# Prompt's squares moved earlier on ScalarE, and one two-bank PSUM tile for the transposes of both attention heads

## The chip, the cores and the metric

The kernel runs on one core of a Trainium2 chip. The metric is the device time of one execution in microseconds. Before the change the median of three runs was 2239.68 us (2239.0 to 2242.85). What follows rests on one profiled execution of the kernel before.

Engine names are those of the profile: PE (TensorE), PEld (its weight loads), DVE (VectorE), ACT (ScalarE), POOL (GpSimd), SP (SyncE, which issues the DMAs).

## The reference, cut to what matters

One layer of a hybrid encoder runs over two groups of tokens with the same weights: a prompt of 512 tokens and a sample of 1024.

```
h = rms_norm(x, norm1_g)                  # x * rsqrt(mean(x*x) + eps) * g
z = h @ w_in                              # conv, pooling, short conv, q, k, v, gates
pooling branch: windowed means of z_b over time, minus z_b;
                p = einsum(p, pool_w) * pool_scale
attention:      s = q k^T + bias on an 8-row by 16-column neighbourhood
                o = softmax(s) v
x = x + (sum_i sigmoid(gate_i) * branch_i) @ w_o
x = x + (val * silu(gate)) @ w_down       # from rms_norm(x, norm2_g) @ w_up
y = rms_norm(x, final_g)
```

Everything is float32; a product is made of three matmuls over a high and a low part of each operand.

## The kernel before, in words

Tokens are cut into three chunks of 512: chunk 0 is the prompt, chunks 1 and 2 the sample. Channels stand on the 128 partitions, so x of one chunk is eight tiles of 128x512 (index k). `split` (L113 to L115) makes the high part with an ACT copy or cast and the low part with a DVE subtraction; `mm3` (L121 to L125) issues the three matmuls of one product, L123, L124 and L125.

**The opening stage.** ACT and DVE split the first weights and prompt's x (`rh`, `rl`). `more_w` (L368) loads and splits two more weight tiles (`m0`, `m1`), and the loop over t the two raw tiles of the value weights into `vwh` and `vwl` (L400 to L405), each of which is made of a half from either raw tile. `square` (L381 to L388) squares one x tile on ACT and adds it to a running sum on POOL (on DVE for chunk 1 and k over 4); the sums are `sq` of a chunk for k 0 to 3 and for k 4 to 7. `rms_scale` (L138 to L152) has PE add these over the partitions with matmuls one column wide (`rb`, L142), then DVE makes the reciprocal root with ten small operations on 128x4 (`rs_v`, `rs_y`, `rs_t`), and a diagonal tile `dg`; `spread` (L156) sends that through PE to all partitions. PE meanwhile multiplies prompt's unnormalised x by the four query and key weights (`zt`), then by the value weights (`zv`, four tiles of 24 matmuls), and scales afterwards. The sample's chunks are normalised first (`norm`, L423 to L426).

**The middle stage.** A plan (L555 to L813) lists twelve column tiles of `w_in`; each is 24 matmuls (`z`) for each of the chunks 1, 2 and 0, followed by an evacuation. Between the z tiles `pump` (L548) puts attention's steps, 24 in all: 4 column blocks of 3 query blocks for 2 pairs of heads. A step makes for each of its two heads the scores `s` on PE, adds the bias and takes the maximum on DVE (L615), exponentials on ACT (L621), a reciprocal on DVE, the scaling on ACT (L624), two or three transposes on PE into a PSUM tile `tp` (L627), and the split into `ph` and `pl`; then PE multiplies by the values (`o`, L634 to L636). The pooling branch (L678 to L725) evacuates its z tiles into `xb`, makes windowed sums on DVE over 1,560 or so columns (`pa`, `pb`), and PE multiplies each chunk by `pool_w` (`pm`, L720); ACT scales that into `ob`. There are two such branches, the second with two levels of sums more.

**PSUM.** Eight banks of 128x512: here four for `z` in rotation (`ztile`), two for `s` and `o`, and two in the pool `mps`, used in turn by `tp` and `pm`.

**The order.** The program is written in one order, and a list scheduler then lays out one queue for each engine, with its own idea of when each operand and buffer is ready; `tc.high_priority()` puts some parts ahead. Each engine works off its queue as laid out.

Of the kernel before, what the change touches and what calls it, by code (L numbers as in the profile page):

```python
# [12 lines left out]
F32 = mybir.dt.float32  # L13
# [4 lines left out]
PSUM = bass.MemoryType.PSUM  # L18
# [46 lines left out]
def encoder(ctx, tc, xT, w_in, w_out, w_o, w_up, w_dn, par, rrel, outT):  # L65
# [122 lines left out]
    with ExitStack() as outer:  # L188
# [140 lines left out]
        with ExitStack() as pha:  # L329
# [59 lines left out]

            more_w(0, 13, HD**-0.5)  # L390
            for k in range(4):
                load_x(k, 1)
            more_w(1, 15, None)
            SP.dma_start(pt, par[:, NG:])
            for k in range(4, KT):
                load_x(k, 1)
            for k in range(KT):
                square(k, 1)
            vw = [[tt(f"vw{m}{a}", F32R) for a in range(4)] for m in "hl"]
            for t in range(2):  # L400
                raw = wp.tile([P, DM], F32, tag="wraw", name=f"wr_v{t}")
                SP.dma_start(raw, w_in[16 + t])
                for a in range(4):
                    hi, lo = (vw[m][a].rearrange("p (k t d) -> p k t d", k=2, t=2)[:, :, t, :] for m in range(2))
                    split(hi, lo, raw[:, a * 256 : (a + 1) * 256].rearrange("p (k d) -> p k d", k=2))  # L405
            for k in range(KT):
                square(k, 0)
            for k in range(KT):
                load_x(k, 2)

# [116 lines left out]
        with ExitStack() as p1:  # L527
                open_zps(4)
                sps = pool(p1, "sps1", 2, space=PSUM)
                mps = pool(p1, "mps1", 2, space=PSUM)  # L530
                bigp = pool(p1, "bigp", 3, side="right")
                gop = pool(p1, "gop", 5, side="right")
                att = p1.enter_context(ExitStack())
# [29 lines left out]
                def attention_pair(p):  # L563
                    t = {}

                    def step(base, r0, kr0, nk, rmi, j):
                        qh, ql, kh, kl, R = (t[x] for x in ("qh", "ql", "kh", "kl", "R"))
                        nt = nk // 4
                        n = nk * 32
                        qc = (base + r0 * GW) // C  # L570
                        qcols = slice(qc * C + j * P, qc * C + (j + 1) * P)
                        k0 = base + kr0 * GW
                        nm = f"{p}{qc}{j}"
                        if j == 0:
                            t["ot"] = ap.tile([P, C], F32, tag="ot", name=f"ot{p}{qc}")
                        ot = t["ot"]

                        def win(x):
                            return x[:, k0 : k0 + nk * GW].rearrange("p (r c) -> p r c", c=GW)[
                                :, :, CB[j] : CB[j] + 32  # L580
                            ]

                        vv = ap.tile([P, 3, 2 * P], F32R, tag="vv", name=f"vv{nm}")
                        g0 = k0 // GW
                        for r in range(4):
                            SP.dma_start(
                                vv[r * 32 : (r + 1) * 32, :nt].bitcast(F32),
                                vt_d[g0 + r : g0 + nk : 4, CB[j] : CB[j] + 32, p * 2 * P : (p + 1) * 2 * P].rearrange(
                                    "i c d -> c i d"
                                ),  # L590
                            )

                        ph = ap.tile([P, 3, 2, P], F32R, tag="ph", name=f"ph{nm}", bufs=1)
                        pl = ap.tile([P, 3, 2, P], F32R, tag="pl", name=f"pl{nm}", bufs=1)
                        for hh in range(2):
                            rows = slice(hh * HD, (hh + 1) * HD)
                            sp = sps.tile([P, C], F32, tag="s", name=f"s{nm}{hh}")
                            so = sp[:, :n]
                            PE.matmul(so, qh[rows, qcols], win(kh)[rows], start=True, stop=False)
                            PE.matmul(so, qh[rows, qcols], win(kl)[rows], start=False, stop=False)  # L600
                            PE.matmul(so, ql[rows, qcols], win(kh)[rows], start=False, stop=True)
                            bm = ap.tile([P, 12, 32], F32, tag="bm", name=f"bm{nm}{hh}")
                            bmv = bm[:, :nk, :]
                            t0 = (kr0 - r0 + 4) * 31 + (CB[j] - 16 * j + 16)
                            rv = R[:, hh, t0 : t0 + 31 * nk]
                            rv = bass.AP(rv.tensor, rv.offset, [list(rv.ap[0]), [31, nk], [1, 32]])
                            cm = pcols("cm", 32 * j, 32)
                            G.tensor_tensor(bmv, rv, cm[:, None, :].broadcast_to([P, nk, 32]), ALU.add)  # L608
                            if rmi is not None:
                                rm = pcols("rm", 12 * rmi, 12)  # L610
                                G.tensor_tensor(bmv, bmv, rm[:, :, None].broadcast_to([P, nk, 32]), ALU.add)
                            s = ap.tile([P, 384], F32, tag="s", name=f"se{nm}{hh}")
                            sv = s[:, :n]
                            mx = small.tile([P, 1], F32, tag="mx", name=f"mx{nm}{hh}")
                            V.tensor_tensor_reduce(  # L615
                                sv, so, bmv.rearrange("p a b -> p (a b)"), 1.0, -3e38, ALU.add, ALU.max, mx
                            )
                            nmx = small.tile([P, 1], F32, tag="nmx", name=f"nx{nm}{hh}")
                            V.tensor_scalar(nmx, mx, -1.0, None, ALU.mult)
                            sm = small.tile([P, 1], F32, tag="sm", name=f"sm{nm}{hh}")  # L620
                            S.activation(sv, sv, AF.Exp, bias=nmx, accum_out=sm)  # L621
                            ri = small.tile([P, 1], F32, tag="ri", name=f"ri{nm}{hh}")
                            V.reciprocal(ri, sm)
                            S.activation(sv, sv, AF.Copy, scale=ri)  # L624
                            tp = mps.tile([P, C], F32, tag="m", name=f"tp{nm}{hh}")
                            for i in range(nt):
                                PE.transpose(tp[:, cols(i)], s[:, cols(i)], ident)  # L627
                            tv = tp[:, :n].rearrange("p (t q) -> p t q", q=P)
                            split(ph[:, :nt, hh, :], pl[:, :nt, hh, :], tv)
                        o = sps.tile([P, C], F32, tag="s", name=f"o{nm}")  # L630
                        ov = o[:, 0:256]
                        for i in range(nt):
                            a, b = (x[:, i].rearrange("p a b -> p (a b)") for x in (ph, pl))
                            PE.matmul(ov, vv[:, i, :P], a, start=(i == 0), stop=False)  # L634
                            PE.matmul(ov, vv[:, i, :P], b, start=False, stop=False)
                            PE.matmul(ov, vv[:, i, P:], a, start=False, stop=(i == nt - 1))  # L636
                        for hh in range(2):
                            rows = slice(hh * HD, (hh + 1) * HD)
                            dst = ot[rows].rearrange("p (r c) -> p r c", c=GW)[:, :, 16 * j : 16 * j + 16]
                            src = o[rows, hh * P : (hh + 1) * P].rearrange("p (r c) -> p r c", c=16)  # L640
                            (S.copy if hh else V.tensor_copy)(dst, src)

                        if j == 3:
                            SP.dma_start(bs_d[3, p, qc], ot)

                    def start():
                        for n in "qk":
                            for m in "hl":
                                t[n + m] = (qp if n == "q" else kp).tile([P, T], F32R, tag=n, name=f"{n}{m}{p}")
                                SP.dma_start(t[n + m].bitcast(F32), qk_d[n, p, m])  # L650
                        t["R"] = ap.tile([P, 2, RL], F32, tag="R", name=f"R{p}", bufs=1)
                        SP.dma_start(t["R"], rrel[p])

                    then(start)
                    kinds = [(0, 0, 0, 8, None), (SEQ_P, 0, 0, 12, 0), (SEQ_P, 8, 4, 12, 1)]
                    for kd in kinds:
                        for j in range(4):
                            then(lambda kd=kd, j=j: bg.append(lambda: step(*kd, j)))
# [19 lines left out]
                def pool_branch(i):  # L678
# [14 lines left out]
                    def sums():  # L693
# [22 lines left out]
                            )  # L716
                        pw = pcols("pw", i * P, P)
                        for c in range(NC):
                            m = mps.tile([P, C], F32, tag="m", name=f"pm{i}{c}")
                            PE.matmul(m, pw, s_lo[:, OFF[c] : OFF[c] + C], start=True, stop=True)  # L720
                            o = go(f"ob{i}{c}")
                            S.activation(o, m, AF.Copy, scale=pc("ps", i))
                            SP.dma_start(bs_d[1, i, c], o)
# [703 lines left out]
```

## Time and profile before

| what | value |
|---|---|
| median of three runs | 2239.68 us |
| the profiled execution | 2238.61 us |
| its span | 2236.8 us |
| PE busy | 2192.5 us, 98% |
| DVE busy | 1353.6 us, 61% |
| ACT busy | 774.7 us, 35% |
| POOL busy | 613.7 us, 27% |
| mean granted clock of PE | 0.992 |

Busy time of PE is a sum over instructions that overlap, so the pitch from one start to the next tells more than a duration. The granted clock is 1.00 at 2.4 GHz and 0.50 at 1.2 GHz. In a timeline, the bracket at the end of a row is the idle time of the engine before it and what ended it.

### The profile page before, as it was taken

Reading aid. Unit: us, or ns where it says so; the run is one execution under the profiler, and the core shown is the slowest. Engines: PE = TensorE matmul, PEld = TensorE weight load, DVE = VectorE, ACT = ScalarE, POOL = GpSimd, SP = SyncE. Lnnn points to the kernel's source line nnn. Section 1 sums busy time; section 2 is a strip of 40 time slices with the busy share of each in tenths; the row PEclk is TensorE's granted clock in tenths of the full one; section 3 lists DMA queues with packets and bytes.
Section 4 is the critical chain, followed back from the end, with each engine's and each line's share of the span. In section 5 each row is a group of like instructions: output and inputs, shape, how many; then the busy total and the mean of one; then the engine's idle time right before and its main releaser. Section 6 shows DMA issues by size and latency. Waiting matters only on the chain.

```text
span 2236.8 us, 26947 instructions
## 1 busy us (share of the span) xinstructions
PE 2192.5 (98%) x9898; PEld 1785.0 (80%) x9898; DVE 1353.6 (61%) x1968; ACT 774.7 (35%) x1316; POOL 613.7 (27%) x701
## 2 busy tenths in 40 slices
PE   8999999999999999999998999999999999999997
PEld 6886767888888778787876888888888887888886
DVE  6635553466666542778158988888777875341414
ACT  5335453333333353303133433333333334221112
POOL 3113343211211210353234544444334430000001
PEclk9999999999999999999998999999999999999999
DMA  5482322622322323874434111211111225432221
GB/s 206 172 294 68 124 77 79 237 84 87 118 79 92 104 99 117 291 252 141 125 112 153 58 67 66 66 57 62 67 62 52 67 80 184 141 123 58 88 86 48
DMA packets 112564, 253.89 MB, mean 114 GB/s; under 512 B 12848, under 2 KB 23600, under 8 KB 109360
## 3 DMA queue, kind: packets, MB, share of 16 engines
q1 hardware_dynamic: 112432, 252.17, 33.6%
q8 instruction: 78, 1.28, 0.2%
q14 instruction: 54, 0.44, 0.1%
HBM read 167.44 MB, written 84.68 MB: 113 GB/s over the span
## 4 chain that ended last, share of the span: by engine, by line
PE 51%; DVE 2%; issue 0%; POOL 0%; ACT 0%; POOLq 0%; DVEq 0%; ACTq 0%
PE yp L124 5%; PE yp L125 5%; PE yp L123 5%; PE ppu L123 4%; PE ppu L124 4%; PE ppu L125 4%; PE o L124 2%; PE o L125 2%; PE o L123 2%; PE p3T L124 1%; PE p3T L123 1%; PE p3T L125 1%; PE p1T L124 1%; PE p1T L125 1%; PE p1T L123 1%; PE p22T L125 1%
## 5 line engine op out<-in xcount | busy, mean ns | idle before, releaser
L123 PE MATMUL yp<-fs,wdhi 128*128 128x512 f32 x480 | 187.2, 392 | 2.4 <-ACT fs L114 2.4
L124 PE MATMUL yp<-fs,wdhi 128*128 128x512 f32 x480 | 188.0, 392 | 0.3 <-DVE fs L115 0.3
L125 PE MATMUL yp<-fs,wdlo 128*128 128x512 f32 x480 | 187.7, 391 | 0.0
L115 DVE TENSOR_TENSOR fs<-fr,fs 128x512 fp32r<-128x512 f32 x63 | 43.4, 691 | 180.0 <-ACT fs L114 180.0
L1198 POOL TENSOR_TENSOR u<-u,u 128x512 f32<-128x512 f32 x63 | 97.6, 1549 | 193.9 <-DVE u L1191 136.3
L847 DVE SCALAR_TENSOR_TENSOR acc<-glu,pt,acc 128x1552 f32<-128x1552 f32 x60 | 109.8, 1830 | 0.7
L1291 POOL TENSOR_TENSOR x<-x,rs 128x256 f32<-128x256 f32 x11 | 7.6, 725 | 371.1 <-DVE acc L1279 367.5
L123 PEld LDWEIGHTS yp<-fs,wdhi 128*128 128x128 f32 x480 | 90.2, 188 | 22.1 <-ACT fs L114 2.8
L114 ACT CAST fs<-fr 128x512 fp32r<-128x512 f32 x63 | 39.0, 621 | 197.7 <-PE yp L125 103.1
L124 PEld LDWEIGHTS yp<-fs,wdhi 128*128 128x128 f32 x480 | 90.6, 189 | 20.0 <-DVE fs L115 1.0
L125 PEld LDWEIGHTS yp<-fs,wdlo 128*128 128x128 f32 x480 | 90.7, 189 | 19.1
L1191 DVE SCALAR_TENSOR_TENSOR u<-c,pt,u 128x512 f32<-128x512 f32 x88 | 100.4, 1179 | 0.0
L253 POOL TENSOR_TENSOR Sg<-wr_g 128x512 f32<-128x512 f32 x16 | 21.4, 1335 | 285.3 <-DMA wr_g<-in_w_in 158.4
L1190 DVE SCALAR_TENSOR_TENSOR u<-c,pt,u 128x512 f32<-128x512 f32 x88 | 86.9, 1025 | 0.0
L608 POOL TENSOR_TENSOR bm<-R,pt 128x384 f32<-128x384 f32 (+1 forms) x48 | 48.0, 1002 | 122.6 <-DVE mx L615 113.5
L1197 ACT ACTIVATE u<-u 128x512 f32<-128x512 f32 x66 | 41.8, 634 | 112.5 <-DVE u L1191 112.5
L123 PE MATMUL z<-hh,wh_i 128*128 128x512 f32 x192 | 78.3, 408 | 0.0
L124 PE MATMUL y<-bl,wh_wo 128*128 128x512 f32 x192 | 75.4, 393 | 2.8 <-DVE bl L115 2.8
L124 PE MATMUL z<-hl,wh_i 128*128 128x512 f32 x192 | 76.3, 398 | 0.0
L125 PE MATMUL z<-hh,wl_i 128*128 128x512 f32 x192 | 76.3, 398 | 0.0
L124 PE MATMUL o<-ml,wh_o 128*128 128x512 f32 x192 | 75.1, 391 | 1.2 <-DVE ml L115 1.2
L123 PE MATMUL o<-mh,wh_o 128*128 128x512 f32 x192 | 75.4, 392 | 0.0
(511 smaller groups left out, 6572.4 us busy)
## 6 DMA issues: line engine op xcount, KB each, us to landing
g<-gate_d SPq DMA_DIRECT2D x24, 1024.0 KB, 5.3
wr_u<-in_w_up SPq DMA_DIRECT2D x44, 512.0 KB, 3.5
f_d<-u SPq DMA_DIRECT2D x66, 256.0 KB, 2.0
fr<-f_d SPq DMA_DIRECT2D x66, 256.0 KB, 2.7
wr_g<-in_w_in SPq DMA_DIRECT2D x32, 512.0 KB, 4.0
wdr<-in_w_dn SPq DMA_DIRECT2D x23, 512.0 KB, 3.5
gate_d<-gp SPq DMA_DIRECT2D x32, 256.0 KB, 2.0
x<-in_xT SPq DMA_DIRECT2D x24, 256.0 KB, 5.8
```

What stands on the lines that cost most here:

```text
L114: S.copy(hi, src)
L115: V.tensor_tensor(lo, src, hi.bitcast(F32), ALU.subtract)
L123: PE.matmul(ps, w[0][:, ws], x[0], start=first, stop=False, **kw)
L124: PE.matmul(ps, w[0][:, ws], x[1], start=False, stop=False, **kw)
L125: PE.matmul(ps, w[1][:, ws], x[0], start=False, stop=last, **kw)
L253: G.tensor_tensor(t, x, y, op)
L608: G.tensor_tensor(bmv, rv, cm[:, None, :].broadcast_to([P, nk, 32]), ALU.add)
L847: keep(V.scalar_tensor_tensor(a, g, w, a, ALU.mult, ALU.add))
L1190: V.scalar_tensor_tensor(b, r[:, 0:C], pc("fc", f * 3), b, ALU.mult, ALU.add)
L1191: V.scalar_tensor_tensor(b, r[:, 2 : C + 2], pc("fc", f * 3 + 2), b, ALU.mult, ALU.add)
L1197: S.activation(ug, ug, AF.Silu)
L1198: (V if j == NJ - 1 else G).tensor_tensor(uv, uv, ug, ALU.mult)
```

## The change: what it does

In the opening stage the prompt's eight squares (`square(k, 0)`), which stood behind the splits of the value weights, now stand four behind the first and four behind the second of the `more_w` tiles, ahead of the squares of chunk 1.

In attention, the transposes of both heads of a step go into one tile `tp` of two banks, and stand together behind the softmax of both heads; the two splits follow. The pool `mps` then holds one such tile, and `pm` takes its PSUM tile from the four `z` banks.

```diff
             more_w(0, 13, HD**-0.5)
             for k in range(4):
+                square(k, 0)
+            for k in range(4):
                 load_x(k, 1)
             more_w(1, 15, None)
             SP.dma_start(pt, par[:, NG:])
             for k in range(4, KT):
                 load_x(k, 1)
+            for k in range(4, KT):
+                square(k, 0)
             for k in range(KT):
                 square(k, 1)
...
-            for k in range(KT):
-                square(k, 0)
             for k in range(KT):
                 load_x(k, 2)
...
-                mps = pool(p1, "mps1", 2, space=PSUM)
+                mps = pool(p1, "mps1", 1, space=PSUM)
...
+                        ss = []
                         for hh in range(2):
...
                             S.activation(sv, sv, AF.Copy, scale=ri)
-                            tp = mps.tile([P, C], F32, tag="m", name=f"tp{nm}{hh}")
+                            ss.append(s)
+                        tp = mps.tile([P, 2, C], F32, tag="m", name=f"tp{nm}")
+                        for hh in range(2):
                             for i in range(nt):
-                                PE.transpose(tp[:, cols(i)], s[:, cols(i)], ident)
-                            tv = tp[:, :n].rearrange("p (t q) -> p t q", q=P)
+                                PE.transpose(tp[:, hh, cols(i)], ss[hh][:, cols(i)], ident)
+                        for hh in range(2):
+                            tv = tp[:, hh, :n].rearrange("p (t q) -> p t q", q=P)
                             split(ph[:, :nt, hh, :], pl[:, :nt, hh, :], tv)
...
-                            m = mps.tile([P, C], F32, tag="m", name=f"pm{i}{c}")
+                            m = ztile(f"pm{i}{c}")
```

No instruction is added or taken away on any engine; their order changes. On PE, at the end of the first pooling branch, this stands before the change (z_2 belongs to the column tile that follows the branch, s and tp to attention, pm to the branch):

```order
L124 MATMUL z_2_2299<-hl_2_1072,wh_i_1895 128x512
L125 MATMUL z_2_2299<-hh_2_1071,wl_i_1896 128x512
L123 MATMUL z_2_2299<-hh_2_1088,wh_i_1895 128x512
L124 MATMUL z_2_2299<-hl_2_1089,wh_i_1895 128x512
L720 MATMUL pm_2186<-pa_2172,pt 128x512
L720 MATMUL pm_2191<-pa_2172,pt 128x512
L720 MATMUL pm_2196<-pa_2172,pt 128x512
L599 MATMUL s_2264<-kh_1624,qh_1620 128x384
L600 MATMUL s_2264<-kl_1626,qh_1620 128x384
L601 MATMUL s_2264<-kh_1624,ql_1622 128x384
L125 MATMUL z_2_2299<-hh_2_1088,wl_i_1896 128x512
```

Between the end of the branch's own z_0 and this first pm stand 38 z matmuls of the next column tile (24 of z_1 and 14 of z_2). At the same place in the changed kernel, on PE (s_2126 is preceded by s_2109, and that by the end of z_0):

```order
L604 MATMUL s_2126<-kh_1624,ql_1622 128x384
L632 MATMUL tp_2143<-pt,se_2116 128x128 x3
L632 MATMUL tp_2143<-pt,se_2133 128x128 x3
L640 MATMUL o_2154<-ph_2107,vv_2102 128x256
L602 MATMUL s_2235<-kh_1624,qh_1620 128x384
L603 MATMUL s_2235<-kl_1626,qh_1620 128x384
L604 MATMUL s_2235<-kh_1624,ql_1622 128x384
L726 MATMUL pm_2180<-pa_2166,pt 128x512
L641 MATMUL o_2154<-pl_2108,vv_2102 128x256
```

Seven more o, the other two pm and then the 24 of z_1 follow. No z matmul of the next column tile stands ahead of the pm any more. It is the same at the second branch, where 55 z matmuls stood between z_0 and the first pm before, and none now.

On DVE in the opening stage, before the change, this stands around the small operations for chunk 1 (vwl is the low part of the value weights, from the raw tiles wr_v_328 and wr_v_338; rb_1 and rb_0 are PE's sums for the chunks 1 and 0):

```order
L115 TENSOR_TENSOR vwl_324<-wr_v_328,vwh_320 128x2x128
L388 TENSOR_TENSOR sq_14_309<-sq_14_309,sq_17_317 128x512
L115 TENSOR_TENSOR vwl_325<-wr_v_328,vwh_321 128x2x128
L115 TENSOR_TENSOR vwl_324<-wr_v_338,vwh_320 128x2x128
L145 TENSOR_SCALAR rs_v<-rb_1_480 128x4
L115 TENSOR_TENSOR vwl_326<-wr_v_328,vwh_322 128x2x128
L131 TENSOR_SCALAR rs_y<-rs_v 128x4
L115 TENSOR_TENSOR vwl_325<-wr_v_338,vwh_321 128x2x128
```

In the changed kernel, on DVE at the same place (the raw tiles are wr_v_350 and wr_v_360):

```order
L115 TENSOR_TENSOR vwl_347<-wr_v_350,vwh_343 128x2x128
L145 TENSOR_SCALAR rs_v<-rb_1_480 128x4
L145 TENSOR_SCALAR rs_v<-rb_0_508 128x4
L131 TENSOR_SCALAR rs_y<-rs_v 128x4
L115 TENSOR_TENSOR vwl_348<-wr_v_350,vwh_344 128x2x128
L131 TENSOR_SCALAR rs_y<-rs_v 128x4
L133 SCALAR_TENSOR_TENSOR rs_t<-rs_y 128x4
L115 TENSOR_TENSOR vwl_349<-wr_v_350,vwh_345 128x2x128
L133 SCALAR_TENSOR_TENSOR rs_t<-rs_y 128x4
L134 TENSOR_TENSOR rs_t<-rs_t,rs_v 128x4
L115 TENSOR_TENSOR vwl_346<-wr_v_360,vwh_342 128x2x128
```

The second half of the first value weights (the row that reads wr_v_360) stood ahead of the operations that wait for PE, and now stands behind nine rows of which the first waits for PE's sums of chunk 1; the small operations of both chunks alternate. Elsewhere: POOL's nine additions for the chunks 0 and 1 had chunk 1's three first and have them last; PE's sums rb_0 go ahead of all but one of rb_1; on SP the first raw value weights go ahead of the loads of chunk 1's x, where they stood behind four of them.

## Rows read from the trace of the kernel before

**Rows 1.** The page, part 1: busy time of PE.

```profile
PE 2192.5 (98%) x9898; PEld 1785.0 (80%) x9898; DVE 1353.6 (61%) x1968; ACT 774.7 (35%) x1316; POOL 613.7 (27%) x701
```

**Rows 2.** Waits of PE in the whole span: total us, times, longest us.

```profile
PE rb L142 <- POOL sq L388: 3.3, 1, 3.3
PE tp L627 <- ACT se L624: 2.7, 7, 0.6
PE pm L720 <- DVE pa L713: 0.2, 1, 0.2
```

**Rows 3.** Timeline of PE, opening stage: start us, us, instruction, [idle before <- releaser].

```profile
24.52 0.39 PE L123 MATMUL zt<-rh,m1h 128*128 128x512 f32 x1
24.75 0.39 PE L124 MATMUL zt<-rl,m1h 128*128 128x512 f32 x1
29.75 1.62 PE L142 MATMUL rb<-ones,sq 128*128 128x1 f32 x14
35.27 0.59 PE L142 MATMUL rb<-ones,sq 128*128 128x1 f32 x2 [3.32 <-POOL sq L388]
...
46.84 1.98 PE L156 MATMUL rb<-dg,ones 128*128 128x512 f32 x4
52.48 0.28 PE L465 MATMUL zv<-vwh,rl 128*128 128x256 f32 x1
52.60 0.39 PE L123 MATMUL zt<-hh,wh_q 128*128 128x512 f32 x1
53.41 0.49 PE L123 MATMUL zt<-hh,m0h 128*128 128x512 f32 x1 [0.42 <-DVE x L424]
54.64 0.50 PE L124 MATMUL zt<-hl,wh_q 128*128 128x512 f32 x1 [0.74 <-DVE hl L115]
```

**Rows 4.** Short windows, opening stage: busy times by engine, then PEclk, DMA share.

```profile
32.25:32.50 0.25, 0.00 (x0) 0.00 (x0) 0.25 (x1) 0.25 (x2) 0.17 (x2) 1.00 0.00 0
32.75:33.00 0.25, 0.00 (x0) 0.00 (x0) 0.25 (x1) 0.25 (x2) 0.25 (x1) 0.50 0.00 0
39.50:40.00 0.50, 0.50 (x5) 0.31 (x4) 0.43 (x3) 0.00 (x0) 0.18 (x1) 1.00 0.82 74
```

**Rows 5.** Timeline of ACT, opening stage.

```profile
16.13 1.15 ACT L118 ACTIVATE m0h<-wr_m 128x512 fp32r<-128x512 f32 x2 [1.30 <-DMA wr_m<-in_w_in]
29.82 4.26 ACT L383 ACTIVATE sq<-x 128x512 f32<-128x512 f32 x8
```

**Rows 6.** Timeline of POOL, opening stage.

```profile
21.83 4.03 POOL L388 TENSOR_TENSOR sq<-sq,sq 128x512 f32<-128x512 f32 x3 [21.39 <-ACT sq L383]
31.04 8.63 POOL L388 TENSOR_TENSOR sq<-sq,sq 128x512 f32<-128x512 f32 x6 [5.18 <-ACT sq L383]
```

**Rows 7.** Timeline of DVE, opening stage.

```profile
16.80 1.29 DVE L119 SCALAR_TENSOR_TENSOR m0l<-wr_m,m0h 128x512 fp32r<-128x512 f32 x2 [1.15 <-ACT m0h L118]
28.41 0.76 DVE L115 TENSOR_TENSOR vwl<-wr_v,vwh 128x256 fp32r<-128x256 f32 x2
32.53 1.23 DVE L131 TENSOR_SCALAR rs_y<-rs_v 128x4 int32<-128x4 int32 x1
41.69 0.17 DVE L131 TENSOR_SCALAR rs_y<-rs_v 128x4 int32<-128x4 int32 x1
```

**Rows 8.** Timeline of DVE, first pooling branch, its start and end.

```profile
205.22 0.69 DVE L687 TENSOR_TENSOR xb<-z,rbp 128x512 f32<-128x512 f32 x1 [1.10 <-PE z L125]
217.76 1.83 DVE L713 SCALAR_TENSOR_TENSOR pa<-pb,pt,xb 64x1552 f32<-64x1552 f32 x1
```

**Rows 9.** Timeline of PE where the first pooling branch ends.

```profile
219.77 2.97 PE L720 MATMUL pm<-pa,pt 128*128 128x512 f32 x6
```

**Rows 10.** Timeline of DVE, second pooling branch, its start and end.

```profile
264.70 0.69 DVE L687 TENSOR_TENSOR xb<-z,rbp 128x512 f32<-128x512 f32 x1 [1.11 <-PE z L125]
280.37 2.15 DVE L713 SCALAR_TENSOR_TENSOR pa<-pb,pt,xb 64x1552 f32<-64x1552 f32 x1
```

**Rows 11.** Timeline of PE where the second pooling branch ends.

```profile
282.57 1.98 PE L720 MATMUL pm<-pa,pt 128*128 128x512 f32 x4 [0.15 <-DVE pa L713]
```

## Prediction

> **What bounds the kernel now.** I read the busy times first: PE is busy for 98% of the span [rows 1]. So whatever makes PE wait lengthens the program by as much, and an edit off PE is worth only what PE waits for it. The second view is therefore the list of PE's waits [rows 2]. Two entries are what the two edits touch: 3.3 us once, for prompt's sums of squares on POOL, and 2.7 us in seven waits of transposes for ACT's scaling, none above 0.6 us. PE waits 0.2 us in all for the pooling branch. Third come the timelines of the opening stage and of the two pooling branches; fourth the order in which the changed kernel's instructions stand, since it decides what waits behind what.
>
> **The opening stage.** Before, PE starts its last 24 key matmuls at 24.52 us, 0.23 us apart, and then waits 3.32 us until 35.27 [rows 3], because POOL adds chunk 1's squares from 21.83 and prompt's only from 31.04 [rows 6], ACT having begun those at 29.82 [rows 5]. The wait costs more than itself: the granted clock, 1.00 at 32.25 to 32.50, stands at 0.50 (1.2 GHz) at 32.75 to 33.00 and is back at 1.00 at 39.5 [rows 4]. So PE works from 35.27 to about 39.4, some 4.1 us, at half speed, which costs half of that, 2.05 us.
>
> After, ACT can start prompt's squares when the first extra weights are done, at 16.13 + 1.15 = 17.28, with 4.26 / 8 = 0.53 us each [rows 5]. POOL starts when two are there, at 18.4, and adds nine times in a row, chunk 1 last. One addition is 4.03 / 3 = 1.34 to 8.63 / 6 = 1.44 us [rows 6], nine are 12.1 to 13.0, so chunk 1's sum is there at 30.5 to 31.4; I take 30.8. PE comes to it after 23 matmuls, at 24.52 + 23 x 0.23 = 29.8, and waits 1.0. Nine sums of 1.62 / 14 = 0.12 us [rows 3], one key and two value matmuls and the last seven sums follow: 1.0 + 0.3 + 0.3 + 0.8, so PE is through with both chunks' sums at 33.2.
>
> There a new wait stands, the one that the DVE order shows. The second half of the first value weights' low part is queued behind an operation that waits for PE's last sum, and PE's next matmul needs it. In between stand seven small operations, 0.2 us apart (0.17 each once POOL is quiet; 1.23 while it adds), and three low parts of 0.76 / 2 = 0.38 us [rows 7]: 1.4 + 1.1 = 2.5, with a semaphore 2.6. PE resumes at 35.8. The value matmuls are 0.12 us apart (52.48 to 52.60 [rows 3]); DVE delivers the further halves every 0.8 us for six of them, 0.72. The 46 left of the first two value tiles take 5.7. A wait of 2.6 after a wait of 1.0 and small sums is so near to the one of 3.3 that I charge the same clock loss, 2.05: PE is there at 43.6. The two spreads take 1.9 (1.98 in the row at 46.84), two value tiles 48 x 0.12 = 5.8, and chunk 1's products start at 51.3. Before they start at 52.60 and then wait 0.42 and 0.74 [rows 3], in effect 53.8; after, DVE has normalised chunk 1 by about 51, as PE gets there, so I count those waits as gone. Gain: 53.8 - 51.3 = 2.5 us. Its ends are 4.6 (no fall of the clock) and 0 (the clock falls, and POOL and the normalisation are 1.2 us later each).
>
> On SP the first raw value weights now stand ahead of chunk 1's loads and wait for a buffer until DVE's low part of the first extra weights is done, 16.80 + 1.29 = 18.09 [rows 7]. That holds the x loads, and ACT still waits for data there. It costs nothing as long as POOL is busy with prompt's sums, until 18.4 + 6 x 1.36 = 26.6; beyond that it moves the end one for one, inside the bound above.
>
> **Attention's transposes.** Same count, same operations, and mostly z matmuls between scores and transposes as before. The first head's split now waits for the transposes of both heads, but five more z matmuls stand between the last transpose and `o`, 5 x 0.23 = 1.2 us, which covers it. I count 0; from below, if all seven waits went, -2.7, and from above a rival.
>
> **The pooling branches.** Here `pm` takes a bank of `z`, and the order on PE has changed most: between the end of the branch's z_0 and its first `pm` nothing stands but a step of attention. `pm` needs the whole of DVE's windowed sums. Before, these run from 205.22 to 217.76 + 1.83 = 219.59 [rows 8], 14.4 us, and PE's first `pm` starts at 219.77 [rows 9]; the second time from 264.70 to 280.37 + 2.15 = 282.52, 17.8 us [rows 10], and `pm` at 282.57 [rows 11]. DVE's queue holds the same rows in that stretch after the change, give or take a 0.3 us copy and a 0.55 us low part, so the stretch stays 14.3 and 18.4 us long by my count. What hid it was PE's own work: 38 z matmuls, 38 x 0.23 = 8.6 us, and 55, 12.5 us. These now come after `pm`. The rest (scores, transposes, `o`) is the same on both sides, but at the first branch eight `o` also move behind the first `pm`, 0.9. Added: 8.6 + 0.9 - 0.3 = 9.2 us, and 12.5 + 0.5 = 13.0 us; together 22.2. Seen as idle time, PE should stand still for 11 to 15 us at each place, in pieces, each ended by attention's chain or by `pa`.
>
> So long a stop brings the clock down, as 3.3 us did. I charge what [rows 4] showed, 4.1 us of work at half speed after each: 2 x 2.05 = 4.1. `pm` is in that work. The ends are 0 and twice this.
>
> One rule decides whether this is a loss at all. The row at 35.27 [rows 3] shows PE waiting 3.32 us for a sum, with value matmuls behind it whose weights' first low parts DVE had finished at 28.41 + 0.76 = 29.2 [rows 7]: nothing overtook. The Trainium skill ("TensorE: Matmul & The Clock Gate", Step-by-step: what each phase is for) says the same, that weight loads may be pulled ahead while matmuls stay in program order. If they could pass, the z matmuls would fill the stop and only the opening gain would be left, about 2237 us; that is the second rival below.
>
> **The sum.** -2.5 + 22.2 + 4.1 = +23.8 us. The profiled execution took 2238.61 us, 1.07 below the median of the runs, so +23.8 makes 2262.4 of it and 2263.5 of the median. I predict 2263.5 us, 1.1% slower.
>
> **The rivals.**
> - *Every step pays.* With both heads in one tile, each of the 24 steps waits for the slower softmax and for six transposes, at the most that a wait costs now, 0.6 us [rows 2]: 24 x 0.6 = 14 us more, 2278. For it: the split has lost its overlap with the second head. Against: the extra z matmuls before `o`.
> - *The stop is worth nothing.* At the branches matmuls go past the waiting `pm`, or the sums on DVE are done when PE gets there, which decides as soon as they take less than the 2 to 3.5 us of attention work in between. Then only the opening's 2.5 is left: 2237, faster. For it: `pm` waits 0.2 us now. Against: that is so only because of 8.6 and 12.5 us of z work in front, and the row at 35.27.
> - *Half a stop.* DVE gets through the sums a third faster, as evacuations and weight splits come later with PE standing: 4.8 and 5.9 us less, 2253. Against: the order puts the same rows between the first and the last sum.
> - *The change doesn't do what it says.* ACT's squares stay bound by loads; then the opening gains 0: 2266, inside the range.
>
> **How the numbers follow.** Forecast (with the last rival in it) 0.74, every step 0.13, half a stop 0.09, nothing 0.04. The range: from no clock loss, the larger opening gain and 2 us less at the branches, +15.5, to twice the clock loss, no gain and 4 us of further waits, +35: 2255 to 2275. The measurement tells about 0.2%, 4.5 us, from no change. Faster by that needs the stop to be worth nothing and the larger gain, 0.03; within it 0.02; slower 0.95.
>
> **What would show it.** In the opening: POOL's nine additions without a gap from about 18.4 to 31; no wait for prompt's sums; a wait of about 2.6 us of a value matmul on a DVE low part; chunk 1's products from about 51. At the branches: PE's idle time 10 us or more twice between 195 and 290 us, with `pm` waiting for `pa`, and PEclk at 0.50 about there. I am wrong if `pm` waits less than 5 us at either place, if transposes wait more than 0.6 us in most steps, or if the time stays under 2250.

## The result, and the profile after

The changed kernel took 2268.5 us (median; 2265.4 to 2269.0), the kernel before 2240.1. The ratio is 1.0115, 95% interval 1.0103 to 1.0127: slower by 1.0 to 1.3% (the quotient of the two medians is 1.0127). Forecast were 2263.5 us and 2255 to 2275. The profiled execution's span is 2266.3 us, 29.5 more than before.

To see where these 29.5 us come from, I put the first start of the same tile of the two traces side by side (tile views, us):

| Tile | before | after | later by |
|---|---|---|---|
| first product of chunk 1 (zt) | 52.6 | 52.5 | -0.1 |
| xb of pooling branch 1 | 205.2 | 204.2 | -1.0 |
| xb of pooling branch 2 | 264.7 | 274.3 | +9.6 |
| first yg, behind all of attention | 410.5 | 435.0 | +24.5 |
| first y | 903.0 | 927.3 | +24.3 |
| first p1T | 1224.1 | 1253.3 | +29.2 |
| end of the span | 2236.8 | 2266.3 | +29.5 |

So the opening gave 1.0 us, the first branch cost 10.6 and the second 14.9, and 5.0 came in a part of the program where PE, DVE, ACT and POOL have their instructions in the same order in both traces.

The waits of PE after the change (whole program; who waited for whom, us in total, times, the longest) answer to [rows 2]:

```profile
PE tp L632 <- ACT se L627: 11.6, 6, 4.7
PE o L640 <- ACT ph L114: 3.9, 2, 2.2
PE pm L726 <- DVE pa L719: 2.7, 1, 2.7
PE zv L466 <- DVE vwl L115: 1.8, 1, 1.8
PE s L602 <- ACT ot L647: 1.4, 1, 1.4
PE rb L142 <- POOL sq L388: 1.4, 1, 1.4
```

PE's wait for POOL's sums shrank from 3.3 us (prompt's) to 1.4 (chunk 1's, which POOL now adds last), and a wait of 1.8 us for `vwl` is new. Transposes wait only six times, but for up to 4.7 us. These long waits are where the branches are. PE's busy time, granted clock and DMA traffic in the two windows of the branches, before and then after:

```profile
200.00:240.00 40.00, 38.19 (x182) 1.00 0.28 90
240.00:300.00 60.00, 59.13 (x280) 1.00 0.35 115
```

```profile
200.00:240.00 40.00, 30.59 (x135) 0.83 0.20 65
240.00:300.00 60.00, 50.04 (x218) 0.83 0.36 115
```

PE stands 9.4 us in the first window and 10.0 in the second (1.8 and 0.9 before), and what it does there it does partly at half clock. PE's rows with a wait, and `pm`, in branch 1 (start, us, line, operation, times, idle time before and its releaser) answer to [rows 9]:

```profile
207.25 0.44 PE L602 MATMUL s<-kh,qh 64*128 64x384 f32 x1 [1.40 <-ACT ot L647]
212.71 0.90 PE L632 MATMUL tp<-pt,se 128*128 128x128 f32 x3 [4.66 <-ACT se L627]
215.30 0.90 PE L632 MATMUL tp<-pt,se 128*128 128x128 f32 x3 [1.68 <-ACT se L627]
217.87 0.58 PE L640 MATMUL o<-ph,vv 128*128 128x256 f32 x1 [1.67 <-ACT ph L114]
219.63 2.07 PE L726 MATMUL pm<-pa,pt 128*128 128x512 f32 x2
222.81 1.88 PE L726 MATMUL pm<-pa,pt 128*128 128x512 f32 x4
```

And in branch 2, answering to [rows 11]:

```profile
278.85 0.90 PE L632 MATMUL tp<-pt,se 128*128 128x128 f32 x3 [3.38 <-ACT se L627]
281.04 0.90 PE L632 MATMUL tp<-pt,se 128*128 128x128 f32 x3 [1.29 <-ACT se L627]
284.19 0.58 PE L640 MATMUL o<-ph,vv 128*128 128x256 f32 x1 [2.24 <-ACT ph L114]
291.76 5.49 PE L726 MATMUL pm<-pa,pt 128*128 128x512 f32 x6 [2.68 <-DVE pa L719]
```

`pm` itself waits 0 and 2.7 us. The idle time stands in front of the attention rows between z_0 and `pm`, each waiting for its softmax; when they are through, `pa` is ready or nearly so. Read by `pm`'s own wait, the stop would look small.

The opening's PE rows after, answering to [rows 3]:

```profile
31.27 2.17 PE L142 MATMUL rb<-ones,sq 128*128 128x1 f32 x18 [1.35 <-POOL sq L388]
33.87 2.32 PE L142 MATMUL rb<-ones,sq 128*128 128x1 f32 x14
37.93 0.58 PE L466 MATMUL zv<-vwl,rh 128*128 128x256 f32 x1 [1.75 <-DVE vwl L115]
45.07 1.88 PE L156 MATMUL rb<-dg,ones 128*128 128x512 f32 x4
```

PE's busy time and, behind it, the granted clock there (the window's length stands first), answering to [rows 4]:

```profile
32.00:34.00 2.00, 2.00 (x18) 1.00 0.48 154
34.00:36.00 2.00, 2.00 (x15) 0.65 0.00 0
36.00:38.00 2.00, 0.25 (x2) 0.50 0.00 0
40.00:42.00 2.00, 2.00 (x14) 0.65 0.00 0
```

The clock fell at 34.6 us, while PE was busy with sums of one column and not in a wait, and was back at 41.4. In the kernel before it fell at 32.6, inside the wait.

### The profile page after: what moved, and what is told of

Same layout as the page of the kernel before. It is cut to its first block, busy times and chain, and to the rows that moved or that the text cites. A ratio compares the mean times of both kernels' runs of the same rounds, so it can differ in the third digit from the quotient of the medians.

```text
span 2266.3 us, 26927 instructions
## 1 busy us (share of the span) xinstructions
PE 2205.4 (97%) x9898; PEld 1795.9 (79%) x9898; DVE 1350.5 (60%) x1968; ACT 777.5 (34%) x1316; POOL 614.8 (27%) x701
## 3 DMA queue, kind: packets, MB, share of 16 engines
q1 hardware_dynamic: 112432, 252.17, 33.2%
## 4 chain that ended last, share of the span: by engine, by line
PE 49%; DVE 3%; issue 0%; POOL 0%; ACT 0%; POOLq 0%; DVEq 0%; ACTq 0%
PE yp L124 5%; PE yp L125 5%; PE yp L123 5%; PE ppu L125 3%; PE ppu L124 3%; PE ppu L123 3%; PE o L124 2%; PE o L125 2%; PE o L123 2%; PE p3T L124 1%; PE p3T L123 1%; PE p3T L125 1%; PE p1T L124 1%; PE p1T L125 1%; PE p1T L123 1%; PE p4B L125 1%
## 5 line engine op out<-in xcount | busy, mean ns | idle before, releaser
L123 PE MATMUL y<-bh,wh_wo 128*128 128x512 f32 x192 | 75.6, 395 | 1.2 <-DVE g L1006 1.2
```

Of the source, the lines that this page charges most:

```text
L123: PE.matmul(ps, w[0][:, ws], x[0], start=first, stop=False, **kw)
```

## The experiments

### The two parts apart

The squares alone, with attention and `pm` as before:

```
 more_w(0, 13, HD**-0.5)
+for k in range(4): square(k, 0)
...
 for k in range(4, KT): load_x(k, 1)
+for k in range(4, KT): square(k, 0)
...
-for k in range(KT): square(k, 0)
```

> The kernel before with the prompt's squares moved as in the change, and nothing else. Theory A (the opening gives what the trace after shows there): first product of chunk 1 no later, branch 1's STT chain about 1.0 us earlier than before, the time 2239 us (-1.0; between -2.5 and 0). Rival (the about 5 us that the trace after lost between 927 and 1253 us, where no order changed, come from the opening's part, by another layout of buffers or another phase of the clock): 2244 us, and y's first product to p1T's first row takes 326 us where before it took 321.

Measured: ratio 0.9988 (0.9978 to 0.9997), 2.7 us faster. It was run once more later:

> The first experiment (the prompt's squares moved, nothing else) run again beside these two, since its gain of 2.7 us stands near the noise. If the opening's gain is real: ratio 0.9975 to 0.9997, chunk 1's first product at 52 to 53 us (half-clock stretch of 6.6 us as in the changed kernel) or at 54.3 again (about 10 us). If it was chance: ratio 0.9997 to 1.001.

The second time: 0.9992 (0.9983 to 1.0000), 1.8 us. So the opening's part is worth about 2 us. Chunk 1 started at 54.3 and 56.2 us in these two traces and at 52.5 in that of the changed kernel, whose opening is the same, because the half-clock stretch lasted longer: 10.2 and 13.7 us for 6.8.

Attention's part alone (joint tile, `pm` from z's pool, squares as before):

```
-mps = pool(p1, "mps1", 2, space=PSUM)
+mps = pool(p1, "mps1", 1, space=PSUM)
...
-tp = mps.tile([P, C], F32, tag="m", name=f"tp{nm}{hh}")
+tp = mps.tile([P, 2, C], F32, tag="m", name=f"tp{nm}")
...
-m = mps.tile([P, C], F32, tag="m", name=f"pm{i}{c}")
+m = ztile(f"pm{i}{c}")
```

> The kernel before with the joint transposes' tile and pm's tiles out of z's pool, the squares left where they were. Theory A (pm standing ahead of the next column's z is the whole loss): branch 1 costs about 10.6 us and branch 2 about 14.9, as in the trace after; the time is 2266 us (+25.5) if the late 5 us belong to the opening's part, 2271 us (+30.5) if they belong to the shift by the attention part. Rival (the opening part does the harm): under 2245 us.

Measured: ratio 1.0106 (1.0092 to 1.0121), 23.8 us slower. The branches cost 10.6 and 15.0 us in its trace, as in the changed kernel. The loss is attention's.

### `pm`'s place or the joint tile

Only `pm` in z's pool; the transposes keep a tile of one bank for each head:

```
-m = mps.tile([P, C], F32, tag="m", name=f"pm{i}{c}")
+m = ztile(f"pm{i}{c}")
```

> The kernel before with nothing changed but pm's tile, which is taken from z's pool; the transposes keep a tile for each head, of one bank, the squares stay where they were. Theory A (pm in z's rotation): branches 1 and 2 together lose 20 to 26 us as in the change, the time is 2262 to 2271 us. Rival (the loss is that of the joint tile, which makes a step's transposes wait for both heads): the time stays within 5 us of before, 2240 to 2245 us.

Measured: ratio 1.0095 (1.0081 to 1.0108), 21.3 us slower; the branches cost 9.2 and 13.9 us. The one line carries nearly the whole loss.

The converse, the changed kernel with `pm` in the transposes' two-bank tile:

```
-m = ztile(f"pm{i}{c}")
+if c != 1: mm = mps.tile([P, 2, C], F32, tag="m", name=f"pm{i}{c}")
+m = mm[:, c % 2]
```

> The changed kernel with pm's results taken from the two-bank tile of the transposes (pm 0 and pm 1 in the two halves of one tile, pm 2 in the next), so that z's pool is left to z; the joint transposes and the moved squares stay. Theory A (the loss is pm in z's rotation): PE has the next columns' z ahead of pm again, branches 1 and 2 cost 0, the time is 2239 us (2236 to 2243). Rival (the joint tile costs each of the 24 attention steps something, .6 us by the longest old wait): 2253 us or more, and PE's waits for se spread over all steps.

Measured: ratio 1.0010 (1.0001 to 1.0019), 2.2 us slower; 24 us came back. But with the opening's gain it should have been faster than before: between xb of branch 1 and yg it lost 4.6 us, though PE's waits for `se` were 2.1 us in both branches, against 1.6 before. Neither theory has that.

The same with `pm` in the pool of the scores:

```
-m = ztile(f"pm{i}{c}")
+m = sps.tile([P, C], F32, tag="s", name=f"pm{i}{c}")
```

> The changed kernel with pm's results taken from the pool of the scores (two banks) and not from z's; joint transposes and moved squares stay. Theory A (the loss comes of z's next tiles standing behind pm, whichever pool pm is taken from otherwise): PE again has the next column's z ahead of pm, the branches lose 2 to 7 us as with pm in the transposes' tile, the time is 2240 to 2250 us. Rival (pm must not share with attention, any pool of attention is as bad, since a score then waits for pm): 2255 us or more, with PE's waits for s's tiles in the branches.

Measured: ratio 1.0020 (1.0011 to 1.0028), 4.5 us slower, 4.3 us lost in the same stretch. Which other pool `pm` goes to makes little difference.

And `pm` in z's pool, but written behind the next column's z (in outline, the first branch; the second likewise):

```
-m = ztile(f"pm{i}{c}")        (leaves sums for mix0)
+mix0 = pool_branch(0)
 cb[1][1]()
+mix0()                         (the three pm)
```

> The changed kernel with pm still in z's pool, but its three products written one column tile later in the program (behind all z of the column that follows each branch), so that z's tiles are taken first and pm comes when its sums are long done. Theory A (it is the place of pm in z's rotation, not the sharing of the pool): PE's wait for pa is gone, the branches lose under 6 us (the joint tile's share, 2.5 to 5 us), the time is 2240 to 2248 us. Rival (z needs all four banks whatever the place of pm): the loss stays near 20 us, 2260 us or more.

Measured: ratio 1.0019 (1.0008 to 1.0030), 4.3 us slower, 3.0 us lost between xb of branch 1 and yg. PE's waits in that trace between 195 and 300 us are

```profile
PE tp L632 <- ACT se L627: 1.8, 2, 1.3
PE s L602 <- DVE mx L618: 0.2, 1, 0.2
```

against 11.0 and 2.7 for `se` and `pa` in the changed kernel. So z's pool can hold `pm`; what costs is its place in front of the next z.

### What the joint tile costs

By an estimate from the windows, 1.7 of the 4.6 us are half of a stretch of 3.4 us at half clock (215.4 to 218.8 us), in which PE was busy throughout. The scores' rows go with the rest. First before, then with the joint tile (start, us, operation, times):

```profile
255.83 0.45 PE L599 MATMUL s<-kh,qh 64*128 64x384 f32 x2
256.11 0.35 PE L600 MATMUL s<-kl,qh 64*128 64x384 f32 x2
256.29 0.35 PE L601 MATMUL s<-kh,ql 64*128 64x384 f32 x2
```

```profile
231.24 0.44 PE L602 MATMUL s<-kh,qh 64*128 64x384 f32 x1
231.52 0.34 PE L603 MATMUL s<-kl,qh 64*128 64x384 f32 x1
231.70 0.34 PE L604 MATMUL s<-kh,ql 64*128 64x384 f32 x1
```

Each head uses 64 of PE's rows. In 11 of the 14 steps of the kernel before in which the six matmuls of the two heads follow each other, the rows have the heads in turn and they run two at a time: all six within 0.74 us (255.83 to the next row at 256.57). Where something stands between, one head's three take as long. In the other 3 of the 14, the rows have the three of one head first, and the six take 1.23 us (237.25 to 238.48); the second of these two rows of the kernel before is the second head's first:

```profile
237.71 0.34 PE L601 MATMUL s<-kh,ql 64*128 64x384 f32 x1
237.75 0.45 PE L599 MATMUL s<-kh,qh 64*128 64x384 f32 x1
```

With the joint tile the heads' scores lie apart more often: six stand next to each other 4 times with `pm` out of z, 12 in the changed kernel and 14 before. PE's busy time in scores alone, 150 to 420 us, of before, of the changed kernel and of the one with `pm` in the transposes' tile:

```profile
150.00:420.00 270.00, 27.46 (x144) 1.00 0.38 124
```

```profile
150.00:420.00 270.00, 32.00 (x144) 0.94 0.29 90
```

```profile
150.00:420.00 270.00, 34.16 (x144) 0.99 0.36 119
```

That is 6.7 us more from the first to the last, for 4.6 lost. The kernel with `pm` one column later has 7.7 more and lost 3.0, so the two do not go one for one. The last experiment tried it from the other side: `o` leaves the scores' pool, so that its two banks are left to the two heads (on top of the wide sums below, with `pm` and transposes as before):

```
-o = sps.tile([P, C], F32, tag="s", name=f"o{nm}")
+o = mps.tile([P, C], F32, tag="m", name=f"o{nm}")
```

> The kernel with moved squares and wide sums, with o taken from the transposes' pool and not from the scores', so that the two banks of the scores' pool are left to scores: the six score matmuls of the two heads stand next to each other on PE in 18 of 24 steps (14 in the kernel before, 12 in the changed one, 4 with the joint tile and pm kept out of z). Theory A (six next to each other run as three pairs, one head in each half of PE's rows, as the rows with x2 show: three such rows take 0.74 us for both heads, and 0.74 us for one head where the heads stand apart; the loss of the joint tile is that of such pairs): the rows with x2 rise from 33 to 50 or so, the scores' time on PE from 25.0 us to about 22, and the time falls by 2 to 4 us against the kernel with wide sums, to a ratio of 0.9948 to 0.9960. Rival (a step's length is set by the chain of softmax, and a pair only makes PE wait later; or o now holds up transposes): ratio 0.9966 or above, PE's waits for se, ph or pl grown by as much as the pairs save.

Measured: ratio 0.9953 (0.9937 to 0.9968), 10.5 us faster than before. The rows with x2 rose from 33 to 56, and the scores' time fell to

```profile
150.00:420.00 270.00, 22.20 (x144) 1.00 0.38 125
```

From xb of branch 1 to yg it is 3.8 us shorter than the kernel with wide sums alone. The two ratios' intervals overlap (0.9966, 0.9951 to 0.9980, for the wide sums alone), so the gain shows in one trace of each and not in the times.

### The opening: a wait or the clock

The squares moved, and the inverse roots not given priority on DVE, so that all `vwl` stand ahead of them:

```
-with tc.high_priority():
+with tc.high_priority() if first else ExitStack():   (first is false for chunks 0 and 1)
     v = small.tile([P, 4], F32, tag="rs_v", name="rs_v")[:, :nb]
```

> The kernel before with the prompt's squares moved (the first experiment), and the inverse roots of chunks 0 and 1 no longer given priority on DVE, so that the six vwl stand ahead of them. Theory A (PE's new wait of 1.75 us for vwl comes of vwl standing behind rs_v on DVE): that wait is gone, zv starts right behind the one-column sums at about 36.3 to 36.9 us instead of 38.7, and the time falls by 1.5 to 2.5 us more, to 4 to 5 us under before (ratio 0.998). Rival (the stretch is set by the clock, which falls at 34 us either way): PE resumes earlier but at half the rate for longer, no gain over the first experiment (ratio 0.9988); or the roots, now later, hold the first zv's results, and chunk 1 starts later (ratio above 1.000).

Measured: ratio 0.9994 (0.9985 to 1.0002). The wait of 1.75 us is gone and nothing was won. The clock of PE with the squares moved alone, and then with this edit (length, busy time, clock):

```profile
34.00:36.00 2.00, 2.00 (x14) 0.59 0.01 5
36.00:40.00 4.00, 2.25 (x11) 0.50 0.01 2
40.00:44.00 4.00, 4.00 (x21) 0.50 0.00 0
```

```profile
34.00:36.00 2.00, 2.00 (x10) 0.50 0.04 13
36.00:40.00 4.00, 4.00 (x19) 0.50 0.00 0
40.00:44.00 4.00, 4.00 (x22) 0.54 0.00 0
```

PE resumes earlier and works at half clock for longer, 10.2 us (33.5 to 43.7) where it had been 8.5 (a stretch of 10.2 with the wait of 1.75 in it): the rival's case. So the next edit changed what PE does between the waits. The sums are made 128 equal columns wide, only the first of which is read. The program has 16 such sums, and the trace has two records for each, the 32 of the expectation that follows:

```
-PE.matmul(ps[:, b:b+1], s[:, cols(b)], ones[:, 0:1], ...)
+PE.matmul(ps[:, cols(b)], s[:, cols(b)], ones, ...)
```

> The kernel before with the prompt's squares moved, and PE's 32 sums of squares of chunks 0 and 1 made 128 equal columns wide instead of one (the same sums, each written 128 times; the first column is read). Theory A (the granted clock falls at 34 us because PE does only one-column sums from 31.5 to 36.9 us, as the row of 0.50 from 34.7 us on shows it busy and still falling): with wide sums the clock stays at 1.00 or falls for less, at most 1 to 2 us of work are added, chunk 1 starts at 50 to 52 us (54.3 and 52.5 in the two traces with one column), and the time falls to 0.997 to 0.998 of before. Rival (the clock falls for PE's waits of 1.7 us, and what runs between them does not matter): the clock falls as before, for 6.6 to 10 us, the wide sums only add, and the ratio is 0.999 to 1.000.

Measured: ratio 0.9966 (0.9951 to 0.9980), 7.6 us faster than before, though PE waited 2.07 us for POOL. The clock does not fall (length, busy time, clock):

```profile
34.00:36.00 2.00, 2.00 (x20) 1.00 0.10 37
36.00:40.00 4.00, 4.00 (x35) 1.00 0.00 0
40.00:44.00 4.00, 4.00 (x25) 1.00 0.68 232
```

The sums of 128 columns (18 records in 2.27 us, 14 in 1.73) take hardly longer than those of one column at full clock (18 in 2.17 above, 14 in 1.62 in [rows 3]), and chunk 1 starts at 49.0 us. But the edit did more than widen the sums. PE's wait of 1.75 us for `vwl` is gone as well: six `vwl` now stand ahead of the roots on DVE.

```profile
32.33 2.09 DVE L115 TENSOR_TENSOR vwl<-wr_v,vwh 128x256 fp32r<-128x256 f32 x6
36.26 0.23 DVE L149 TENSOR_SCALAR rs_v<-rb 128x4 f32<-128x4 f32 x2 [1.84 <-PE rb L143]
```

So this run alone does not tell the width of the sums from the wait. The next one does, beside the one with the roots not first: neither waits for `vwl`, and only the width differs. With both edits:

> As the kernel with the squares moved and the roots not first (no wait for vwl), with the 32 sums made 128 equal columns wide. Theory A (the clock falls for the one-column sums, so that the wait taken away gave nothing): now no low stretch, or a short one, between 30 and 45 us, chunk 1 starts at 49 to 51 us, ratio 0.996 to 0.998. Rival (the one wait of 1.8 us for POOL at 30 us is enough for the fall): low from about 34 us for 6.6 us or more, ratio 0.999 to 1.000.

Measured: ratio 0.9969 (0.9960 to 0.9979). That is some 5.6 us less than with the roots not first and sums of one column (0.9994, 0.9985 to 1.0002), each against the kernel before beside it, and the intervals do not meet. Here the clock did fall, but for a third of the time, 3.4 us (32.8 to 36.2) for 10.2:

```profile
34.00:36.00 2.00, 2.00 (x10) 0.50 0.01 4
36.00:40.00 4.00, 4.00 (x35) 0.97 0.00 0
```

So in two traces with nearly the same waits (1.83 and 1.99 us for POOL, none for `vwl`) the low stretch was shorter by 6.8 us with the wide sums. The clock can still fall behind the wait for POOL: it did here behind 1.99 us and did not with the wide sums alone behind 2.07, and why stays open. Both edits together win nothing over the wide sums alone.

### The 5 us behind 900 us

> The changed kernel as it is, run again beside the others, for the 5 us that its first trace lost between y's first product (927 us) and p1T's first row (1253 us). Theory A (they are chance of one execution: the opening alone and the attention part alone showed +2.3 and -0.7 us there): the stretch from y to p1T takes 321 to 324 us this time (326.0 in the first trace), and the ratio to the kernel before falls to 1.0105 or so (+23.5 us). Rival (they come of both parts together): 326 us again, and the ratio stays at 1.0115 to 1.0125.

Measured: ratio 1.0110 (1.0095 to 1.0125). From y to p1T it took 325.1 us; neither range has that. In the other traces of this study the stretch takes from 320.4 us (attention's part alone) to 326.3 (squares moved, roots not first, wide sums; attention as before). So it is not the work of both parts together. The rows show what varies. The 20 us around PE's wait for `bl` (2.75 us before, 2.79 after), before and after:

```profile
923.00:943.00 20.00, 17.25 (x70) 0.91 0.76 243
```

```profile
947.30:967.30 20.00, 16.82 (x61) 0.83 0.67 237
```

Nearly the same idle time (2.75 and 3.18 us), but the clock stays down longer behind it. Over nine windows of the 320 us behind y, length times the clock's missing share comes to 8.8 us before, 12.2 and 12.4 in the two traces of the changed kernel, 12.0 in that of 326.3 us, 6.8 with attention's part alone. The 3.4 us more would be PE's loss if it had worked through all of the low time. It worked for 20.3 us of that time after and 15.1 before, and half of the difference, 2.6 us, is the estimate of what the clock cost. PE's idle time in the windows is 1.8 us more (13.5 against 11.7). That tells 4.4 of the 4.9 us between y and p1T. The same two terms tell the stretch in every kernel here: with idle time and half of the work at half clock taken off, it is 301.8 to 303.3 us in all fourteen traces. Part of the 4.9 may be the choice of the execution: the profiled one of the kernel before took 2238.6 us, and the medians of that kernel beside the experiments were 2240 to 2244. Why the same waits bring the clock down for longer in one kernel than in another stays open. The parts' ratios add up to 21 us and the whole was 24.7 and 25.8, each with about 3 us to either side, so the times do not settle it either.

## Why the prediction was right, and where not

- **The stop at the branches** held in mechanism and size: 11.3 us predicted for the first with the clock's loss (9.2 + 2.05), 10.6 measured; 15.05 and 14.9 for the second. The two terms hold apart, too, by an estimate from the windows. Up to the first `pm` PE lost 9.6 and 12.6 us more than before (idle time, and half of what it worked at half clock) for the forecast 9.2 and 13.0; behind it the clock cost 1.3 and 2.8 for 2.05 each. The idle time alone, put at 11 to 15 us at each place, was 9.4 and 10.0, because part of the stop was filled with work at half clock. The single line with `pm` makes it, and a later place for `pm` undoes it. The Trainium skill's sentence that matmuls stay in program order ("TensorE: Matmul & The Clock Gate", Step-by-step: what each phase is for) agrees here: the next column's z, whose high weights ACT had finished at 205.0 us, did not start before 224.13, though PE stood 4.66 us at one stretch. So the rival "the stop is worth nothing" fell. DVE's sums took 15.0 and 17.4 us for 14.4 and 17.8 before, so "half a stop" fell with it.
- **The sign I named for it was wrong.** I wrote that I would be wrong if `pm` waited less than 5 us at either place; it waited 0 and 2.7. The order showed a step of attention between z_0 and `pm`; I should have seen that its waits would come first in the queue and take the idle time. The sum over all waits in the window was the sign to name.
- **The opening** was put at -2.5 us; the trace gave -1.0, the times about -2. POOL's nine additions (17.59 to 31.22; predicted 18.4 to 30.8) came as worked out, PE's wait for them nearly so (1.35 for 1.0), and the new wait for `vwl` was there but shorter (1.75 for 2.6). The step that failed is the one that put the end of the sums at 33.2: PE came through them at 36.2. I had divided the row of 14 by 14 to price one sum, but a sum is two records, and that row is seven sums. Nine sums took 2.03 us (31.27 to 33.30) where I had 1.0, and seven would have taken 1.62 at full clock where I had 0.8: 1.9 of the 3.0 us. POOL's end gave 0.5, and the clock, which fell in the last sums (2.32 us for 1.62), 0.7. The shorter wait took part of this back, and chunk 1 started at 52.5 us for 51.3. The clock's price itself was about right: low for 6.8 us (34.6 to 41.4), of which PE worked 5.1, so 2.5 us by estimate for the 2.05 that I charged.
- **Attention's transposes** were put at 0. The joint tile cost 2.5 us in the two branches between the traces with and without it (25.5 against 23.1; the times, 23.8 against 21.3, are too near each other to tell) and 4.6 in the trace where `pm` kept out of z. It was not the rival's way, more waits in each step, for the transposes' waits outside the branches went down, from 1.1 to 0.6 us. The heads' scores lost their neighbours in the order, which the order could have shown; I looked for waits in it only. That this alone is the joint tile's price is argued from the scores' time and the last experiment, not shown by a run of its own.
- **Nothing** was in the sum for the part behind 900 us, where 5.0 us came. In the traces that is nearly the whole miss (29.5 us for 23.8). By the ratios, the change cost 25.8 and 24.7 us, one to two more than forecast.

## What to carry to other kernels

A small tile taken from a pool that a long stream rotates through stands in that stream's order: what it waits for, the stream waits for, so ask what is next in the pool before asking whether there is room. Look for the idle time over the whole window, not at the instruction that you suspect, since whatever stands ahead of it in the queue shows the waits. A wait that is taken away is worth what the clock lets it be: look at the granted clock of the stretch, and at what PE does between its waits. Before dividing a row's time by its count, ask how many records one instruction leaves: here it was two.

## What the runs showed of the hardware

- The granted clock fell to 0.50 (1.2 GHz) while PE worked through the one-column sums, and stayed low for 6.8 to 13.7 us in the kernels with the same opening. With the same sums 128 columns wide it stayed at 1.00 in two kernels, behind waits of 2.07 and 1.62 us, and fell for 3.4 us in a third behind one of 1.99. The wide sums cost PE 0.1 us more for a row of 14 records (1.73 for 1.62).
- Two matmuls of 64 rows on the two halves of PE ran side by side where the rows have the two heads in turn: six in 0.74 us. Where one head's three came first, the six took 1.23. That matmuls in different row groups overlap is also what the Trainium skill says ("TensorE: Matmul & The Clock Gate", The mechanism). The Trainium skill says as well, in the same section, that matmuls start and end in strict order. In what order the six stand in PE's queue is not on record here, so these rows neither bear that out nor speak against it.
- While POOL added, DVE's subtractions of two tiles took longer: the two `m1l` 3.41 us in the changed kernel for 1.29 in the kernel before, where POOL began only after them (21.83).
